# Recurrence of a hybrid trunk on whole two-head tiles, with its operands made on GpSimd

## Chip, cores and metric

The kernel runs on one core of a Trainium2 chip. The metric is the device time of one execution in microseconds; the number given for a kernel is the median of its runs.

## What is computed

Two layers of one trunk run over 256 context and 512 latent tokens of width 1024. Each layer projects the normalised tokens once and feeds three mixers (attention, a bidirectional recurrence, a short convolution); then comes a mixture of experts. The change concerns the recurrence. For each of 8 heads of width 64 and both directions, token by token:

```python
def step(s, inp):
    wt, kkt, at, kt, vt = inp[:5]
    sa = jnp.einsum('bhvk,bhk->bhv', s, kkt)
    s = s * wt[:, :, None, :] - sa[..., None] * (kkt * at)[:, :, None, :] + vt[..., None] * kt[:, :, None, :]
    y = jnp.einsum('bhvk,bhk->bhv', s, inp[5]) if emit else None
    return s, y
```

`wt` is a decay, `kkt` a normalised removal key, `at` a rate, `kt` and `vt` key and value, the last input the receptance.

## The kernel before

The 768 tokens are cut into 12 chunks of 64. Two heads (a "pair") share the 128 partitions, 64 each, and both directions `d` lie beside each other in a tile; so a layer has 4 pairs x 12 chunks = 48 steps. A step has two parts.

`window` (L639) does what needs no state, three steps ahead of its use. It makes the scaled operands `t1`, `t2` and `kr` on VectorE (L666 to L673), puts keys (`kbd`, L681) and corrections (`cbd`, L682) into two block tiles per direction, and a scaled copy of `kr` into `sv` on GpSimd (L686). Products of `kbd` and `cbd` with `kr` go to PSUM and from there, masked, into `sv` and `sc` (L700 to L709). Four transposes of the block tiles are copied to `tok` (L717 to L719). A ladder of six levels of 16-bit products (L730 to L757) then makes the inverse `xt`.

`chain` (L771) takes the state from chunk to chunk. Value and state rows of both heads lie in `V`. Each head's half is a product of its own with 64 weight columns (L794 to L797): `zz` from `V`; its copy `zr`; `aa` from `xt`; its copy `sa`; a correction of `zz`; a second `zr` and `aa`; V is overwritten (L824); `pss` gives the next state, `yy` the output, again in halves (L829 to L842). The next state is `pss` plus the decayed old one, `sf` from GpSimd (L787, L846).

`rwkv_phase` (L891) calls `ahead`, which moves three windows on by three stages each, then `chain`, then `fill`, which hands out dense projection work (`pw` products, with operands split by ScalarE, L132, and GpSimd, L134) behind marked products of the chain. The order on each engine is fixed when the program is built, by priorities (chain 9000, windows and fill 4000, dense products 0) and a modelled timeline. TensorE, VectorE, ScalarE and GpSimd each run their list in that order. An f32 product appears in the trace as two instructions, so one `mm` of two directions is a group of four.

`value_rows` (L762) copies the value rows of the next chunk into one of three `V` buffers on GpSimd; `readout` (L857) normalises the outputs of a segment on VectorE.

Of the kernel before, what the change touches and what calls it, by code (L numbers as in the profile page):

```python
# [67 lines left out]
class Trunk:  # L68
# [186 lines left out]
    def masks(self, mk):  # L255
# [3 lines left out]
        self.scm = cp.tile([P, 2, 2, P], BF16, name="scm")  # L259
# [5 lines left out]
        same, a, b = (mk.tile([P, P], F32, name=n) for n in ("mk_s", "mk_a", "mk_b"))  # L265
# [9 lines left out]
        blk(same, 6)  # L275

        for d in range(2):
            for m, op in enumerate(((ALU.is_lt, ALU.is_le), (ALU.is_gt, ALU.is_ge))[d]):
                v.tensor_tensor(a, rr, rc, op)
                v.tensor_tensor(self.scm[:, d, m], a, same, ALU.mult)  # L280
        self.scc = cp.tile([P, 2, 2, 64], BF16, name="scc")
        for h in range(2):
            hs = slice(64 * h, 64 * h + 64)
            v.tensor_copy(self.scc[hs], self.scm[hs, :, :, hs])
# [10 lines left out]
    def layer_params(self, l, pp, ps, tag):  # L295
# [24 lines left out]
        v.tensor_copy(a["c1"], cols[:, R_KA:R_KA + 4])  # L320
# [180 lines left out]
    def pair(self, p, full):  # L501
# [55 lines left out]
        def rates(s):  # L557
# [10 lines left out]
            for d in range(2):  # L568
# [16 lines left out]
                v.tensor_scalar(ta[:, d], ta[:, d], 0.5, 0.5, ALU.mult, ALU.add)  # L585
# [53 lines left out]
    def window(self, q, n, emit, kb):  # L639
# [50 lines left out]

        g.sc = rp.tile([P, 2, 2, P], F32, name="sc", tag="sc", bufs=4)
        bank = self.slots[n % 3]
        ps = bank.rearrange("p (t d m i) -> p t d m i", t=2, d=2, m=2)
# [7 lines left out]
        hi = lambda t: t.rearrange("p d m (h i) -> p d m h i", h=2)[:, :, :nm]  # L701
        if emit:
            hi = lambda t: t.rearrange("p d m (h i) -> p (d m) h i", h=2)
            in0 = ps[:, 1].rearrange("p d m i -> p (d m) i")[:, :, None].to_broadcast([P, 4, 2, 64])
            v.tensor_tensor(hi(g.sc), in0, hi(self.scm), ALU.mult)
        else:
            hi = lambda t: t[:, :, 0].rearrange("p d (h i) -> p d h i", h=2)
            in0 = ps[:, 1, :, 0, None].to_broadcast([P, 2, 2, 64])
            v.tensor_tensor(hi(g.sc), in0, hi(self.scm), ALU.mult)  # L709
        if n < NCH - 1:  # L710

            g.tok = rp.tile([P, 2, 2, 64], F32, name="tok", tag="tok", bufs=4)
            pt = bank.rearrange("p (d q x) -> p d q x", d=2, q=4)
            self.mark()
            for d in range(2):
                for t, rows in enumerate((cbd, kbd)):
                    self.tr(bank[:, (2 * d + t) * P:(2 * d + t + 1) * P], rows[:, d])  # L717
            nc.scalar.activation(g.tok[0:64], pt[0:64, :, 0::3], AF.Copy)
            nc.scalar.activation(g.tok[64:128], pt[64:128, :, 2:0:-1], AF.Copy)  # L719
# [51 lines left out]
    def chain(self, q, n, V, emit):  # L771
# [19 lines left out]
        pz = self.psz.tile([P, 2, 2, HD], F32, name="pz", tag="z")  # L791
        zz, aa = pz[:, 0], pz[:, 1]
        self.mark()
        for h, hs in enumerate(halves):  # L794
            first = self.mma(zz[hs, 0], g.sv[:, 0, h, 0], V[:, 0, h], True)
            with tc.issue_after(first.ins):
                self.mma(zz[hs, 1], g.sv[:, 1, h, 0], V[:, 1, h])  # L797
        py = self.psz.tile([P, 2, 2, HD], F32, name="py", tag="y")
        pss, yy = py[:, 0], py[:, 1]
        sa = None  # L800
        for it in range(2):
            r = rp.tile([P, 2, HD], F32R, name="zr", tag="zr", bufs=2)
            if it:
                v.tensor_tensor(r, zz, sa, ALU.subtract)
            else:
                nc.scalar.activation(r, zz, AF.Copy)
# [3 lines left out]
            if not it:  # L810
# [3 lines left out]
                for d in range(2):  # L814
                    self.mma(zz[:, d], g.sc[:, d, 0], sa[:, d])
                if emit:

                    firsts = []
                    for h, hs in enumerate(halves):
                        firsts.append(self.mma(yy[hs, 0], g.sv[:, 0, h, 1], V[:, 0, h], True))  # L820
                        with tc.issue_after(firsts[-1].ins):
                            self.mma(yy[hs, 1], g.sv[:, 1, h, 1], V[:, 1, h])
        for h, hs in enumerate(halves):
            v.tensor_copy(V[hs, :, h], aa[hs])  # L824
# [4 lines left out]
        for h, hs in enumerate(halves):  # L829
            if last:  # L830
                break
            if emit:
                with tc.issue_after(firsts[h].ins):
                    for d in range(2):
                        self.mma(pss[hs, d], g.tok[:, d, h], V[:, d, h])
            else:
                first = self.mma(pss[hs, 0], g.tok[:, 0, h], V[:, 0, h], True)
                with tc.issue_after(first.ins):
                    self.mma(pss[hs, 1], g.tok[:, 1, h], V[:, 1, h])
        if emit:  # L840
            for d in range(2):
                self.mma(yy[:, d], g.sc[:, d, 1], sa[:, d])  # L842
        if not last:
            for h, hs in enumerate(halves):
                if n:
                    v.tensor_tensor(out[hs, :, h], pss[hs], sf[hs], ALU.add)  # L846
                else:
                    v.tensor_copy(out[hs, :, h], pss[hs])
        if emit:
# [4 lines left out]
            nc.scalar.activation(ysl, yy, AF.Copy)  # L854
# [36 lines left out]
    def rwkv_phase(self, full):  # L891
        nc, tc = self.nc, self.tc
        with ExitStack() as st:
# [5 lines left out]
            kb = [[self.rp.tile([P, 2, P], F32, name=f"{n}{a}") for n in ("kbd", "cbd")] for a in range(2)]  # L899
            for t in sum(kb, []):  # L900
# [39 lines left out]
            def ahead(n, steps):  # L940

                for j in range(max(steps)):
                    for a, m in enumerate(steps):
# [3 lines left out]
                        if n + a not in gens:  # L947
                            gens[n + a] = self.window(q, c, full or c >= 4, kb[c % 2])
# [987 lines left out]
```

## Time and profile before

| | before |
|---|---|
| median of 3 runs | 3748.26 us (3740.76 to 3754.14) |
| profiled execution | 3755.7 us, of it span 3753.9 us |
| TensorE busy, weight loads busy | 3485.4 us (93%), 2313.5 us (62%) |
| VectorE, ScalarE, GpSimd busy | 2025.0 (54%), 1284.2 (34%), 893.0 us (24%) |
| mean granted TensorE clock | 0.952 of full speed |

The span runs from the first to the last instruction. PE is TensorE's products, PEld its weight loads, DVE VectorE, ACT ScalarE, POOL GpSimd. Busy is the time in which an engine had at least one instruction in work; a product counts from its start to its last result, so products overlap.

### The profile page before, as it was taken

What the parts mean: (1) busy time and instruction counts of PE and PEld (TensorE: products, weight loads), DVE (VectorE), ACT (ScalarE), POOL (GpSimd) and SP (SyncE); (2) the same over time, 40 slices, a digit from 0 to 9 for tenths busy, and PEclk for the clock granted to TensorE, in tenths of its full rate; (3) what the DMA queues carried; (4) which work ended last, traced back from release to release, by engine and by line L of the source; (5) the groups of instructions that cost most, each with busy time, mean ns of one, the idle gap of its engine ahead of it and who ended that gap; (6) DMA issues with size and microseconds to landing.
All of it is one profiled execution on the core that took longest, in us unless ns stands there. A gap on an engine that the chain in (4) does not pass through costs nothing. (4 is left out here: it accounts for less than half of the span.)

```text
span 3753.9 us, 58688 instructions
## 1 busy us (share of the span) xinstructions
PE 3485.4 (93%) x22479; PEld 2313.5 (62%) x22479; DVE 2025.0 (54%) x4902; ACT 1284.2 (34%) x3145; POOL 893.0 (24%) x1181
## 2 busy tenths in 40 slices
PE   6999999999998998999999899899999989799998
PEld 4777777777987892233333467677777978633442
DVE  6787878773665461121222677878773766412122
ACT  3454444443444211111110344555553452211111
POOL 3333343332320420000000243334343312100000
PEclk9999999999999998999999899898999999899999
DMA  5312031334115435778888411111112135399998
GB/s 177 102 61 95 29 111 49 110 114 150 52 39 183 136 133 211 294 293 310 331 331 328 138 57 29 31 36 38 35 38 92 46 132 186 132 409 409 409 409 351
DMA packets 297053, 621.11 MB, mean 165 GB/s; under 512 B 19258, under 2 KB 160532, under 8 KB 296772
## 3 DMA queue, kind: packets, MB, share of 16 engines
q1 hardware_dynamic: 293028, 605.30, 44.5%
q0 software_dynamic: 1728, 6.29, 0.5%
q10 hardware_dynamic: 2016, 5.77, 0.4%
q8 instruction: 177, 2.90, 0.3%
q14 instruction: 104, 0.85, 0.1%
HBM read 584.00 MB, written 33.29 MB: 164 GB/s over the span
## 5 line engine op out<-in xcount | busy, mean ns | idle before, releaser
L81 PE MATMUL ph<-we,xin 128*64 128x512 f32 x2048 | 514.8, 607 | 7.7 <-DMA we<-in_exp_w 4.7
L81 PE MATMUL pw<-hhi,w_hi 128*128 128x512 f32 (+1 forms) x1272 | 500.0, 397 | 14.5 <-ACT w_hi L132 6.3
L81 PE MATMUL pw<-hlo,w_hi 128*128 128x512 f32 (+1 forms) x1272 | 457.3, 364 | 0.0
L81 PE MATMUL pw<-hhi,w_lo 128*128 128x512 f32 (+1 forms) x1272 | 455.9, 364 | 1.0 <-POOL w_lo L134 1.0
L134 POOL TENSOR_TENSOR w_lo<-w_raw,w_hi 128x1024 fp32r<-128x1024 f32 x124 | 302.3, 2444 | 413.4 <-ACT w_hi L132 340.9
L81 PEld LDWEIGHTS ph<-we,xin 128*64 128x64 f32 x2048 | 151.5, 139 | 330.5 <-issue 315.7
L736 DVE TENSOR_TENSOR wt<-slot,lvm 128x256 f16<-128x256 f32 x576 | 232.8, 418 | 114.3 <-PE slot L81 78.8
L81 PEld LDWEIGHTS pw<-hhi,w_hi 128*128 128x128 f32 x1272 | 245.5, 195 | 55.2 <-ACT w_hi L132 7.6
L81 PEld LDWEIGHTS pw<-hhi,w_lo 128*128 128x128 f32 x1272 | 244.9, 194 | 38.9 <-issue 3.8
L81 PEld LDWEIGHTS pw<-hlo,w_hi 128*128 128x128 f32 x1272 | 246.2, 195 | 32.8 <-issue 13.8
L132 ACT ACTIVATE w_hi<-w_raw 128x1024 fp32r<-128x1024 f32 x168 | 177.1, 1057 | 239.4 <-DMA w_raw<-in_w_in 63.3
L81 PE MATMUL py<-we,hT 128*64 128x512 f32 x1024 | 248.5, 607 | 8.0 <-DMA we<-in_exp_w 2.8
L1791 POOL TENSOR_TENSOR ylo<-y,yhi 128x512 fp32r<-128x512 f32 x28 | 35.3, 1280 | 891.6 <-ACT yhi L1790 891.6
L753 ACT ACTIVATE xx<-slot 128x256 f16<-128x256 f32 x384 | 145.7, 382 | 166.0 <-PE slot L81 154.2
L1801 DVE TENSOR_TENSOR xr<-xr,psc 128x512 f32<-128x512 f32 x144 | 90.3, 682 | 196.6 <-PE psc L81 196.4
L1718 ACT ACTIVATE sl<-ph 64x512 f32<-64x512 f32 x64 | 37.8, 590 | 451.5 <-PE ph L81 431.8
L1719 DVE TENSOR_TENSOR hid<-sl,ph 64x512 f32<-64x512 f32 x64 | 44.2, 690 | 267.2 <-ACT sl L1718 266.7
L81 PE MATMUL slot<-xt,wt 128*128 128x128 f16 x960 | 135.9, 229 | 34.8 <-DVE wt L736 34.3
L81 PEld LDWEIGHTS py<-we,hT 128*64 128x64 f32 x1024 | 70.2, 137 | 151.6 <-issue 132.7
L81 PE MATMUL pt<-w_hi,hhi 128*128 128x256 f32 x544 | 156.2, 289 | 4.8 <-ACT xk L1115 2.0
L768 POOL COPY V<-vt 64x128 f32<-64x128 f32 x192 | 58.1, 305 | 425.3 <-PE py L85 323.0
L81 PE MATMUL pt<-w_lo,hhi 128*128 128x256 f32 x544 | 155.7, 287 | 3.2 <-POOL w_lo L134 3.2
(418 smaller groups left out, 7779.9 us busy)
## 6 DMA issues: line engine op xcount, KB each, us to landing
we<-in_exp_w SPq DMA_DIRECT2D x384, 1024.0 KB
w_raw<-in_w_in SPq DMA_DIRECT2D x124, 512.0 KB
ada_w<-in_ada_w SPq DMA_DIRECT2D x96, 512.0 KB
w_raw<-in_w_branch SPq DMA_DIRECT2D x24, 512.0 KB
w_raw<-in_w_out SPq DMA_DIRECT2D x20, 512.0 KB
gd<-gt SPq DMA_DIRECT2D x24, 384.0 KB
g<-gd SPq DMA_DIRECT2D x24, 384.0 KB
gd<-gt SPq DMA_DIRECT2D x24, 256.0 KB
```

What stands on the lines that cost most here:

```text
L81: return self.leg(self.nc.tensor.matmul(out, lhsT, rhs, start=start, stop=stop))
L132: nc.scalar.activation(hi, raw, AF.Copy)
L134: self.lo_eng.tensor_tensor(lo, raw, hi.bitcast(F32), ALU.subtract)
L736: v.tensor_tensor(wt, ps, self.lvm[:, :, l], ALU.mult)
L753: nc.scalar.activation(x, ps2, AF.Copy)
L768: self.nc.gpsimd.tensor_copy(t[ho, :, h], self.two(q.vt[s][ho], z0, z1))
L1718: nc.scalar.activation(sl, ph[0:64, ns], AF.Silu)
L1719: v.tensor_tensor(hid[0:64, ns], sl, ph[64:128, ns], ALU.mult)
L1791: (v if by_block else self.ylo_eng[nh]).tensor_tensor(lo, yn, hi.bitcast(F32), ALU.subtract)
L1801: v.tensor_tensor(x, x, pt, ALU.add)
```

## The change

The keys and corrections of a direction share one block tile `kc`; `kr` becomes a tile with one block per head, so one product per direction gives both `sv` and `sc`. `kc`, `kr` and `sc` are allocated once and cleared once, where the pool made `kr` and `sc` anew. `t1`, `t2` and `kr` are made on GpSimd. The minus sign of the corrections moves into the rates. In the chain, one product per direction takes `V` of both heads, and the block of interest is copied: `zr` per head (ScalarE and VectorE, the second time both on VectorE), `V` on VectorE and ScalarE, `y` by two ScalarE copies. The diff, cut to its core:

```diff
...
+                for h in range(2):
+                    hs = slice(64 * h, 64 * h + 64)
+                    v.tensor_copy(self.scc[hs, d, m], a[hs, hs])
...
-        v.tensor_copy(a["c1"], cols[:, R_KA:R_KA + 4])
+        v.tensor_scalar(a["c1"], cols[:, R_KA:R_KA + 4], -1.0, None, ALU.mult)
...
-                v.tensor_scalar(ta[:, d], ta[:, d], 0.5, 0.5, ALU.mult, ALU.add)
+                v.tensor_scalar(ta[:, d], ta[:, d], -0.5, -0.5, ALU.mult, ALU.add)
...
-        v.tensor_tensor(t1, t1, at(e3, True), ALU.mult)
+        pl = nc.gpsimd
+        pl.tensor_tensor(t1, t1, at(e3, True), ALU.mult)
         t2 = rp.tile(shp, F32, name="t2", tag="t2")
-        v.tensor_tensor(t2, th, at(e3, True), ALU.mult)
-        kr = rp.tile([P, 2, 2, 64], F32, name="kr", tag="kr", bufs=2)
-        v.tensor_tensor(kr[:, :, 0], kk, at(e, False), ALU.mult)
+        pl.tensor_tensor(t2, th, at(e3, True), ALU.mult)
+
+
+        kc, kr, g.sc = kb
         if emit:
             self.need(q.u["receptance"])
-            v.tensor_tensor(kr[:, :, 1], two(q.r), at(e, True), ALU.mult)
+        for h in range(2):
+            hs = slice(64 * h, 64 * h + 64)
+            pl.tensor_tensor(kr[hs, :, h, 0], kk[hs], at(e, False)[hs], ALU.mult)
+            if emit:
+                pl.tensor_tensor(kr[hs, :, h, 1], two(q.r)[hs], at(e, True)[hs], ALU.mult)
...
-        kbd, cbd = kb
         for h in range(2):
             hs, ho = slice(64 * h, 64 * h + 64), slice(64 - 64 * h, 128 - 64 * h)
-            v.tensor_tensor(kbd[hs, :, ho], two(q.k)[hs], t1[hs], ALU.mult)
-            v.scalar_tensor_tensor(cbd[hs, :, hs], kk[hs], -1.0, t2[hs], ALU.mult, ALU.mult)
-            dst = g.sv[hs, :, h, :nm]
+            v.tensor_tensor(kc[hs, :, ho], two(q.k)[hs], t1[hs], ALU.mult)
+            v.tensor_tensor(kc[hs, :, hs], kk[hs], t2[hs], ALU.mult)
+            dst = g.sv[hs, :, :nm, h]
             if n:
                 f = q.f[hs, :, n - 1, None, None].to_broadcast([64, 2, nm, 64])
-                nc.gpsimd.tensor_tensor(dst, kr[hs, :, :nm], f, ALU.mult)
+                pl.tensor_tensor(dst, kr[hs, :, h, :nm], f, ALU.mult)
             else:
-                nc.gpsimd.tensor_copy(dst, kr[hs, :, :nm])
+                pl.tensor_copy(dst, kr[hs, :, h, :nm])
...
+        ps = bank.rearrange("p (d h m i) -> p d h m i", d=2, h=2, m=2)
         self.mark()
-        for t, lhs in enumerate((kbd, cbd)):
-            for d in range(2):
-                self.mm(ps[:, t, d, :nm], lhs[:, d], kr[:, d, :nm], True, True)
+        for d in range(2):
+            self.mm(ps[:, d, :, :nm], kc[:, d], kr[:, d, :, :nm], True, True)
         for h in range(2):
-            ho = slice(64 - 64 * h, 128 - 64 * h)
-            v.tensor_tensor(g.sv[ho, :, h, :nm], ps[ho, 0, :, :nm], self.scc[ho, :, :nm], ALU.mult)
...
+            hs, ho = slice(64 * h, 64 * h + 64), slice(64 - 64 * h, 128 - 64 * h)
+            v.tensor_tensor(g.sc[hs, :, :nm, hs], ps[hs, :, h, :nm], self.scc[hs, :, :nm], ALU.mult)
+            v.tensor_tensor(g.sv[ho, :, :nm, h], ps[ho, :, h, :nm], self.scc[ho, :, :nm], ALU.mult)
...
+            g.tok = rp.tile([P, 2, P], F32, name="tok", tag="tok", bufs=4)
+                self.tr(bank[:, d * P:(d + 1) * P], kc[:, d])
+            nc.scalar.activation(g.tok, bank[:, 0:256].rearrange("p (d x) -> p d x", d=2), AF.Copy)
...
+        own = list(enumerate(halves))
+        both = lambda t, d: t[:, d, None].to_broadcast([P, 2, HD])
+        pz = self.psz.tile([P, 512], F32, name="pz", tag="z")
+        zz = pz[:, 0:256].rearrange("p (d h x) -> p d h x", d=2, h=2)
+        aa = pz[:, 256:384].rearrange("p (d x) -> p d x", d=2)
+        py = self.psz.tile([P, 2, 2, 2, HD], F32, name="py", tag="y")
+        pss, yy = py[:, 0], py[:, 1]
+
+        def begin(out, lhs):
+
+            first = self.mma(out[:, 0], lhs(0), V[:, 0], True)
+            with tc.issue_after(first.ins):
+                self.mma(out[:, 1], lhs(1), V[:, 1])
+            return first
+
...
+        begin(zz, lambda d: g.sv[:, d, 0])
+        sa = first = None
...
+            for h, hs in own:
+                if it:
+                    v.tensor_tensor(r[hs], zz[hs, :, h], sa[hs], ALU.subtract)
+                elif h:
+                    v.tensor_copy(r[hs], zz[hs, :, h])
+                else:
+                    nc.scalar.activation(r[hs], zz[hs, :, h], AF.Copy)
...
+                    self.mma(zz[:, d], g.sc[:, d, 0], both(sa, d))
...
+                    first = begin(yy, lambda d: g.sv[:, d, 1])
+        for h, hs in own:
+            if h:
+                nc.scalar.activation(V[hs, :, h], aa[hs], AF.Copy)
+            else:
+                v.tensor_copy(V[hs, :, h], aa[hs])
...
+        tok = lambda d: g.tok[:, d]
+        if last:
+            pass
+        elif emit:
+            with tc.issue_after(first.ins):
+                for d in range(2):
+                    self.mma(pss[:, d], tok(d), V[:, d])
+        else:
+            begin(pss, tok)
...
+                self.mma(yy[:, d], g.sc[:, d, 1], both(sa, d))
...
+            for h, hs in own:
...
+                    v.tensor_tensor(out[hs, :, h], pss[hs, :, h], sf[hs], ALU.add)
...
+                    v.tensor_copy(out[hs, :, h], pss[hs, :, h])
...
+            for h, hs in own:
+                nc.scalar.activation(ysl[hs], yy[hs, :, h], AF.Copy)
...
-            kb = [[self.rp.tile([P, 2, P], F32, name=f"{n}{a}") for n in ("kbd", "cbd")] for a in range(2)]
-            for t in sum(kb, []):
+            kc, kr, sc = (
+                [self.rp.tile(shape, F32, name=f"{n}{a}") for a in range(m)]
+                for n, m, shape in (("kc", 2, [P, 2, P]), ("kr", 2, [P, 2, 2, 2, 64]), ("sc", 4, [P, 2, 2, P]))
+            )
+            for t in kr + sc:
...
-                            gens[n + a] = self.window(q, c, full or c >= 4, kb[c % 2])
+                            gens[n + a] = self.window(q, c, full or c >= 4, (kc[c % 2], kr[c % 2], sc[(n + a) % 4]))
```

## Rows read from the trace of the kernel before

**Rows 1.** Stages: busy us (instructions) by engine, PEclk, DMA share, GB/s.
```profile
117.00:899.00 782.00, 740.86 (x5867) 576.92 (x5865) 578.55 (x1500) 361.19 (x1027) 266.05 (x409) 0.97 0.27 87
...
2188.00:2851.00 663.00, 610.67 (x4577) 461.47 (x4574) 506.12 (x1345) 333.68 (x949) 243.60 (x399) 0.93 0.12 37
```
**Rows 2.** First copy of each step, line 806, first layer: ns min/median/max, first and last.
```profile
L806 ACT ACTIVATE zr<-pz x48: 253/277/325, 116.9 to 898.9; 128x128 fp32r<-128x128 f32 x48
```
**Rows 3.** Timeline of one step, 2836 to 2842: start, us, instruction [idle before].
```profile
2836.79 0.60 DVE L824 COPY V<-pz 64x128 f32<-64x128 f32 x2
...
2837.49 0.45 PE L85 MATMUL py<-V,tok 128*64 128x64 f32 x4
...
2838.44 0.39 PE L81 MATMUL pw<-hhi,w_lo 128*128 128x512 f32 x1
...
2838.76 0.31 PEld L85 LDWEIGHTS py<-V,tok 128*64 128x64 f32 x4 [0.36 <-issue]
...
2839.83 0.61 DVE L846 TENSOR_TENSOR V<-py,sf 64x128 f32<-64x128 f32 x2 [2.45 <-PE py L85]
...
2840.17 0.45 PE L85 MATMUL pz<-V,sv 128*64 128x64 f32 x4 [0.26 <-DVE V L846]
...
2841.44 0.13 PEld L85 LDWEIGHTS pz<-V,sv 128*64 128x64 f32 x1 [0.37 <-issue]
```
**Rows 4.** Groups of weight loads, whole run: busy us, mean ns | idle before, releasers.
```profile
L85 PEld LDWEIGHTS pz<-V,sv 128*64 128x64 f32 x768 | 54.5, 142 | 52.6 <-issue 9.6 <-DVE V L848 9.6 <-DVE V L846 8.3
...
L85 PEld LDWEIGHTS pz<-sa,sc 128*128 128x128 f32 x384 | 53.8, 200 | 4.8 <-ACT xt L757 1.5 <-issue 0.8 <-ACT sa L812 0.7
...
L85 PEld LDWEIGHTS py<-V,tok 128*64 128x64 f32 x704 | 51.6, 141 | 35.3 <-issue 11.7 <-DVE V L824 5.2 <-DVE wt L736 4.6
```
**Rows 5.** Timeline of TensorE's products, 400 to 415 us.
```profile
402.81 0.70 PE L81 MATMUL bk<-wal,ups 64*128 64x256 f32 x2
...
406.16 0.46 PE L85 MATMUL py<-V,sv 128*64 128x64 f32 x8
...
407.72 0.27 PE L108 MATMUL slot<-ident,kbd 128*128 128x128 f32 x1
...
409.84 0.61 PE L85 MATMUL pz<-sa,sc 128*128 128x64 f32 x4
...
411.86 0.61 PE L81 MATMUL slot<-kr,cbd 128*128 128x128 f32 x4
```
**Rows 6.** VectorE in the window: groups of the whole run, and one line's ns min/median/max.
```profile
L682 DVE SCALAR_TENSOR_TENSOR cbd<-kk,t 64x128 f32<-64x128 f32 x192 | 92.2, 480 | 19.9 <-PE slot L108 17.9
...
L700 DVE TENSOR_TENSOR sv<-slot,scc 64x256 f32<-64x256 f32 (+1 forms) x192 | 76.6, 399 | 42.9 <-PE slot L81 38.5 <-PE pz L85 0.8 <-ACT sa L827 0.4
...
L705 DVE TENSOR_TENSOR sc<-slot,scm 128x512 f32<-128x512 f32 x80 | 54.5, 682 | 1.4 <-PE py L85 0.5
...
L670 DVE TENSOR_TENSOR kr<-kk,e 128x128 f32<-128x128 f32 x96 | 37.2, 387 | 1.7 <-POOL sv L686 0.2
...
L682 DVE SCALAR_TENSOR_TENSOR cbd<-kk,t x192: 270/290/2532, 99.1 to 2802.4; 64x128 f32<-64x128 f32 x192
```
**Rows 7.** GpSimd products of 128x128 and 64x128: ns min/median/max, first and last start.
```profile
L1132 POOL TENSOR_TENSOR rot<-xq,r_q x32: 445/459/903, 976.3 to 3042.9; 128x128 f32<-128x128 f32 x32
...
L787 POOL TENSOR_TENSOR sf<-V,f x160: 392/399/960, 176.4 to 2841.0; 64x128 f32<-64x128 f32 x160
```
**Rows 8.** Timeline of all engines, 2571 to 2576 us.
```profile
2571.89 2.34 POOL L134 TENSOR_TENSOR w_lo<-w_raw,w_hi 128x1024 fp32r<-128x1024 f32 x1
...
2572.24 2.70 DVE L874 TENSOR_SCALAR var<-var 128x16 f32<-128x16 f32 x1
...
2575.18 0.69 PE L85 MATMUL pz<-V,sv 128*64 128x64 f32 x4 [2.15 <-DVE V L848]
```
**Rows 9.** GpSimd's copy of value rows, second recurrence phase: busy us, mean ns | idle before.
```profile
L768 POOL COPY V<-vt 64x128 f32<-64x128 f32 x90 | 27.7, 307 | 206.5 <-PE py L85 144.6 <-DVE wt L736 22.8 <-DVE V L824 19.7
```

More of the change, by code (lines that the diff above doesn't have):

```diff
@@ L258, in masks @@
         v = nc.vector
-        self.scm = cp.tile([P, 2, 2, P], BF16, name="scm")
         self.lvm = cp.tile([P, 2, 6, P], F16, name="lvm")
@@ L264, in masks @@
         rc, rr, ci, ri = (mk.tile([P, P], I32, name=n) for n in ("mk_c", "mk_r", "mk_ci", "mk_ri"))
-        same, a, b = (mk.tile([P, P], F32, name=n) for n in ("mk_s", "mk_a", "mk_b"))
+        a, b = (mk.tile([P, P], F32, name=n) for n in ("mk_a", "mk_b"))
         nc.gpsimd.iota(rc, pattern=[[1, P]], base=0, channel_multiplier=0)
@@ L273, in blk @@
             v.tensor_tensor(dst, ci, ri, ALU.is_equal)
-        blk(same, 6)
+        self.scc = cp.tile([P, 2, 2, 64], BF16, name="scc")
         for d in range(2):
@@ L279, in masks @@
                 v.tensor_tensor(a, rr, rc, op)
[L280 to L284, printed above, removed]
+                for h in range(2):
+                    hs = slice(64 * h, 64 * h + 64)
+                    v.tensor_copy(self.scc[hs, d, m], a[hs, hs])
         for l in range(6):
@@ L684, in window @@
+            dst = g.sv[hs, :, :nm, h]
             if n:
                 f = q.f[hs, :, n - 1, None, None].to_broadcast([64, 2, nm, 64])
-                nc.gpsimd.tensor_tensor(dst, kr[hs, :, :nm], f, ALU.mult)
+                pl.tensor_tensor(dst, kr[hs, :, h, :nm], f, ALU.mult)
             else:
-                nc.gpsimd.tensor_copy(dst, kr[hs, :, :nm])
+                pl.tensor_copy(dst, kr[hs, :, h, :nm])
         yield
-        g.sc = rp.tile([P, 2, 2, P], F32, name="sc", tag="sc", bufs=4)
@@ L701, in window @@
[L701 to L709, printed above, removed]
+            hs, ho = slice(64 * h, 64 * h + 64), slice(64 - 64 * h, 128 - 64 * h)
@@ L710, in window @@
+            v.tensor_tensor(g.sc[hs, :, :nm, hs], ps[hs, :, h, :nm], self.scc[hs, :, :nm], ALU.mult)
+            v.tensor_tensor(g.sv[ho, :, :nm, h], ps[ho, :, h, :nm], self.scc[ho, :, :nm], ALU.mult)
         if n < NCH - 1:
-            g.tok = rp.tile([P, 2, 2, 64], F32, name="tok", tag="tok", bufs=4)
-            pt = bank.rearrange("p (d q x) -> p d q x", d=2, q=4)
+            g.tok = rp.tile([P, 2, P], F32, name="tok", tag="tok", bufs=4)
             self.mark()
             for d in range(2):
-                for t, rows in enumerate((cbd, kbd)):
-                    self.tr(bank[:, (2 * d + t) * P:(2 * d + t + 1) * P], rows[:, d])
@@ L789, in chain @@
                 )
-        pz = self.psz.tile([P, 2, 2, HD], F32, name="pz", tag="z")
-        zz, aa = pz[:, 0], pz[:, 1]
-        self.mark()
[L794 to L800, printed above, removed]
+        own = list(enumerate(halves))
[10 more added lines that the diff above has]
+            return first
+        self.mark()
+        begin(zz, lambda d: g.sv[:, d, 0])
+        sa = first = None
         for it in range(2):
             r = rp.tile([P, 2, HD], F32R, name="zr", tag="zr", bufs=2)
[L803 to L806, printed above, removed]
+            for h, hs in own:
[5 more added lines that the diff above has]
+                    nc.scalar.activation(r[hs], zz[hs, :, h], AF.Copy)
             self.mark()
@@ L814, in chain @@
                 for d in range(2):
-                    self.mma(zz[:, d], g.sc[:, d, 0], sa[:, d])
+                    self.mma(zz[:, d], g.sc[:, d, 0], both(sa, d))
                 if emit:
[L818 to L824, printed above, removed]
+                    first = begin(yy, lambda d: g.sv[:, d, 1])
[4 more added lines that the diff above has]
+                v.tensor_copy(V[hs, :, h], aa[hs])
         if emit:
@@ L828, in chain @@
         self.mark()
[L829 to L839, printed above, removed]
+        tok = lambda d: g.tok[:, d]
[7 more added lines that the diff above has]
+            begin(pss, tok)
         if emit:
             for d in range(2):
-                self.mma(yy[:, d], g.sc[:, d, 1], sa[:, d])
+                self.mma(yy[:, d], g.sc[:, d, 1], both(sa, d))
         if not last:
-            for h, hs in enumerate(halves):
+            for h, hs in own:
                 if n:
-                    v.tensor_tensor(out[hs, :, h], pss[hs], sf[hs], ALU.add)
+                    v.tensor_tensor(out[hs, :, h], pss[hs, :, h], sf[hs], ALU.add)
                 else:
-                    v.tensor_copy(out[hs, :, h], pss[hs])
+                    v.tensor_copy(out[hs, :, h], pss[hs, :, h])
         if emit:
```

4 lines of the change are left out of this document (removed).

## The prediction

> **What bounds the kernel now.** I read the stages first, then the recurrence inside them, then what its links wait for.
>
> The stage table [rows 1] has one line for each recurrence phase, 117 to 899 us in the first layer and 2188 to 2851 in the second. TensorE is busy for 741 of 782 us and 611 of 663, VectorE for 579 and 506, ScalarE for 361 and 334, GpSimd for only 266 and 244. So TensorE and VectorE are the full engines, and GpSimd has the room. All of the change lies in these two phases, 1445 us together.
>
> A phase is 48 steps (four head pairs, twelve chunks) [rows 2]: 782 us over 47 intervals are 16.6 us a step, 663 are 14.1. TensorE is not 93% full of work, though: a lone small product counts as busy until it has drained, and in these phases dense projection products are put between the links of the chain. The handoffs show what that does [rows 3]. The second V copy ends at 2837.39 (2836.79 + 0.60), but the second half of the state product starts at 2838.76, 1.37 us later, because dense products stand between the halves. The next link has the same shape: the second half of the new state is there at 2840.44, its product starts at 2841.44, 1.00 us later. And each of these second halves has 0.36 or 0.37 us of idle weight load in front of it, put down to "issue". Over the run, the weight loads of `pz<-V,sv` and `py<-V,tok` have 52.6 and 35.3 us of idle in front of them, against 4.8 for the full-width `pz<-sa,sc` [rows 4]. So the step is a chain of short links, each queued in an engine's fixed order; it is not one engine's throughput.
>
> **The change part by part**, per step.
>
> *TensorE, the products with V.* `zz` and `pss` are today two pieces of four instructions, 0.45 us each [rows 3]; each becomes one piece of four with 128 weight columns and 128 moving columns, for which the nearest row is `slot<-kr,cbd`, 0.61 us [rows 5]. That saves 0.29 us twice. `yy` stands in one piece of eight at 0.46 [rows 5] and becomes 0.61: +0.15. Of the idle before the half-width loads, 87.9 us / 96 = 0.92 a step, part is a true wait for V (the rows name it); I take 0.4 off, between 0 and 0.88.
>
> *TensorE, the rest.* The corrections `sc` times `sa` go from 64 to 128 moving columns. At 64 columns four take 0.61 us, and at 128 columns four of `kr,cbd` take 0.61 as well [rows 5]: nothing. The window's eight products of 128 columns become four of 256. Streaming the same columns gives 0 as one end; the other is `bk<-wal,ups`, two of 256 columns in 0.70 [rows 5], so four in 1.40 against 2 x 0.61: +0.2. I take +0.1. Two of four transposes go: (0.61 - 0.27) / 3 = 0.11 between starts [rows 5], so -0.22. The sum for TensorE is -0.58 + 0.15 - 0.4 + 0.1 - 0.22 = -0.95 us, with ends at -1.7 and +0.15.
>
> *The chain.* Each of `zz` and `pss` now waits for both halves and then goes at once. The 1.00 and 1.37 us between the halves can go wholly (-2.4), or not at all if the dense products land in front of the merged product instead. I take -0.9. Against it, the second `zr` is two VectorE copies in a row instead of one (+0.30, half of a pair's 0.60 in rows 3), the V copies run side by side on two engines (-0.30), and three handoffs now need VectorE and ScalarE both free. I take +0.3 for the three, between 0 and +1. Net -0.6.
>
> *VectorE.* Four operand products leave. The nearest rows give 0.39 with its port waits and 0.29 without [rows 6]; 4 x 0.35 = -1.4. The block products are taken from PSUM by four instructions of 0.40 instead of two of 0.40 and one of 0.68 [rows 6]: +0.12. `zr` costs two copies more and V one less: +0.30. That is -1.0. What can eat it is the port: the `cbd` copies take 480 ns in the mean and 290 in the median [rows 6], so four such instructions lose 4 x 0.19 = 0.76 us a step while GpSimd holds SBUF. That loss may stay (0) or double (+0.76); I take +0.2, so VectorE -0.8.
>
> *GpSimd.* Two products of 128x128 at 0.46 and four of 64x128 at 0.40 [rows 7] are 2.5 us a step more. In the second layer it rises from 244 / 48 = 5.1 to 7.6 us of a 14.1 us step. I cost that at nothing: a window begins three steps before it is used. If that cover is gone, its operands come 2.5 - 1.4 = 1.1 us later.
>
> *ScalarE.* One `tok` copy less; one V copy and one `y` copy more: about +0.2 us on an engine that is half idle; nothing. The masks and the cleared tiles are made once a layer, two more `memset` tiles and larger ones: under 3 us a layer on idle GpSimd; nothing. The DMA queues get no instruction more or less.
>
> *The sum.* These do not add up, since each is partly hidden by the others. I take a third of TensorE's 0.95 (the rest becomes waiting), half of the chain's 0.6 (the fixed order can put another product in its place), and a quarter of VectorE's 0.8: 0.3 + 0.3 + 0.2 = 0.8 us a step. Over 96 steps that is 77 us. The profiled execution took 3755.7 us, so 3679; the median of the runs shown, 3748.3, is 7.4 below it, so the forecast is 3671.5 for a median. With all of TensorE's and the chain's share, 1.55 us a step, it would be 149 us, about 3600.
>
> **The rivals.**
>
> *The gain is given back at the handoffs* (chance 0.22). Three links now need a VectorE and a ScalarE copy of the same product. VectorE is three quarters busy and ScalarE half [rows 1], and both work strictly in order, so the later of two queues counts. With +0.9 instead of +0.3, and dense products in front of the merged ones, the chain gains 0 and only TensorE's and VectorE's shares are left, which waiting swallows: 0 to 0.25 us a step, 3725 to 3750. For it: the step is links, not throughput. Against it: the pieces of 0.45 and the idle of 0.36 vanish whatever the copies do. I expect 3740.
>
> *Slower: GpSimd and its port become the bound* (chance 0.22). A VectorE instruction with two SBUF inputs, or one that only scales a small SBUF tile, stands still while GpSimd works: the 128x16 scaling took 2.70 us beside a `w_lo` of 2.34, and the chain's next product waited 2.15 us for the copy behind it [rows 8]. That shows the mechanism already on the chain. The Trainium skill, "SBUF — State Buffer", section "SBUF: two separate sides", has it as a rule that speaks against this change: the port pair is an exclusive lock, held for a whole instruction, and the loser blocks fully. By that rule, the trace agrees (2.70 us for an instruction that is that long only behind the lock). In this kernel it would work so: the four `kc` products come just as GpSimd makes the same window's `kr` and `sv`, each waits for one GpSimd instruction of 0.40 [rows 7], 1.6 us, and holds GpSimd up for 4 x 0.29 = 1.2 us [rows 6]. GpSimd then has 7.6 + 1.2 = 8.8 us a step, and its fixed order parks it: 206.5 us of the second layer, 4.3 us a step, it stands before the V copy of a later step [rows 9]. 8.8 + 4.3 = 13.1 us, just what the shorter step would be (14.1 - 0.8 = 13.3). From there the windows come late and TensorE stands before their products: the window's path is 1.1 + 1.6 = 2.7 us longer, and half of that, less the 0.8 gained, is +0.55 us a step: 3748 + 53 = 3801, about 3795. Against it: the parked time shrinks by itself when GpSimd has something else in front, and VectorE keeps only five such instructions of nine a step.
>
> *The change doesn't do what it says* in one point: the chain's matrix products lose instructions, not columns. That is in the sum already.
>
> **How the numbers follow.** Forecast 3672 (0.56), its own band 3600 to 3725; the handoff rival 3740 (0.22), which covers 3725 to 3760; the port rival 3795 (0.22), from 3760 up. About 0.3%, 11 us, is what a measurement of this kernel can tell from no change, so faster begins below 3737: all of the forecast and nearly half of the handoff rival, 0.66. Same takes the rest of it, 0.12; slower is the port rival, 0.22. The range that holds 8 in 10 leaves out the forecast's lowest end (below 3600, 0.08) and half of the port rival (above 3790, 0.11).
>
> **What would show each step right or wrong.** Right: `pz` and `py` products with V in one piece of four per link, with no "issue" idle before them; the two phases shorter by 35 to 45 us each; VectorE some 40 us less busy in each, GpSimd some 120 us more; `kc` at 480 ns or less in the mean. The port rival would show in `kc` above 700 ns, in long scalings beside GpSimd, and in TensorE waiting for `nb` or `kc`. The handoff rival would show in phases of the old length, with `zr` and V waiting for whichever copy comes second. The forecast is wrong if the phases are not shorter although the pieces merged, or if the gain lies outside 117 to 899 and 2188 to 2851.

## The result and the profile after

The changed kernel takes 3643.94 us (median of 4 runs, 3639.78 to 3644.71) against 3744.70 us for the kernel before on the same chip: a ratio of 0.9722, 95% interval 0.9709 to 0.9734; that is 101 us less by the medians and 104 by the ratio. The profiled execution has a span of 3641.9 us where it was 3753.9.

Busy time over the whole run, from the page of the changed kernel; the clock beside it is 0.963:

```profile
PE 3367.1 (92%) x20863; PEld 2243.8 (62%) x20863; DVE 1950.3 (54%) x4725; ACT 1289.5 (35%) x3233; POOL 1133.7 (31%) x1729
```

The stage table of the changed kernel, for the two recurrence phases (from the first to the last `zr` copy), answers to [rows 1]. Columns: length, then busy time of TensorE, weight loads, VectorE, ScalarE and GpSimd, then granted clock and DMA:

```profile
118.00:845.00 727.00, 689.90 (x5032) 550.63 (x5032) 542.24 (x1419) 366.47 (x1078) 378.71 (x674) 0.99 0.29 94
2138.00:2741.00 603.00, 538.48 (x3775) 414.05 (x3774) 470.82 (x1261) 326.85 (x977) 348.15 (x636) 0.97 0.13 40
sum 1330.00, PE 1228.38 PEld 964.69 DVE 1013.05 ACT 693.32 POOL 726.85; mean PE 614.19 PEld 482.34 DVE 506.53 ACT 346.66 POOL 363.43
```

The phases went from 782 to 727 and from 663 to 603 us. That is 115 us of 1445, or 1.2 us a step, and it is the whole gain: the stretch between them lasts 1293 us, before 1289. VectorE is 36 and 35 us less busy, GpSimd 113 and 105 us more, TensorE 51 and 72 us less. TensorE's idle time did not shrink: 1445 - 1351.5 = 93 us before, 1330 - 1228.4 = 102 now.

TensorE's busy time is not work alone. Its mean granted clock, 0.97 and 0.93 in [rows 1], is now 0.99 and 0.97 in the two phases. In the traces' records of the clock, 140 us of the two phases stood at the lower of its two levels (1.2 of 2.4 GHz) before, in 25 stretches, and 61 us now, in 12; each stretch came behind a time in which TensorE had stood idle in part. At half clock at most half of the time is lost, so by this estimate 70 us were lost before and 31 now: up to 39 of the 115 us can have come by the clock.

The groups of the changed kernel that answer to [rows 4, 6, 7], whole run: busy us, mean ns, idle before and what ended it:

```profile
L81 PE MATMUL slot<-kr,kc 128*128 128x256 f32 (+1 forms) x384 | 97.5, 376 | 1.5 <-ACT xtr L746 1.0
L674 POOL TENSOR_TENSOR kr<-kk,e 64x128 f32<-64x128 f32 x192 | 91.7, 477 | 109.0 <-PE slot L81 78.8 <-DVE kk L545 19.8 <-DVE vt L634 1.9
L684 DVE TENSOR_TENSOR kc<-kk,t 64x128 f32<-64x128 f32 x192 | 78.6, 409 | 5.9 <-POOL t L666 5.4
L683 DVE TENSOR_TENSOR kc<-pk,t 64x128 f32<-64x128 f32 x192 | 78.3, 408 | 16.1 <-PE slot L108 9.6 <-POOL t L664 3.5 <-PE slot L81 0.7
L85 PEld LDWEIGHTS pz<-V,sv 128*128 128x128 f32 x384 | 50.4, 190 | 35.2 <-PE slot L81 24.5 <-DVE V L844 3.4 <-PE py L85 1.9
L85 PEld LDWEIGHTS py<-V,tok 128*128 128x128 f32 x352 | 47.4, 194 | 12.2 <-ACT V L822 10.6 <-issue 0.3
...
L666 POOL TENSOR_TENSOR t<-a,e 128x128 f32<-128x128 f32 x96 | 43.6, 455 | 55.1 <-DVE kc L684 49.8 <-ACT xx L742 2.0 <-ACT sa L827 0.9
L805 DVE CAST zr<-pz 64x128 fp32r<-64x128 f32 x96 | 28.3, 295 | 18.1 <-ACT zr L807 15.5
L822 ACT ACTIVATE V<-pz 64x128 f32<-64x128 f32 x96 | 26.2, 273 | 47.2 <-DVE V L824 45.0
```

The block products are hardly slower beside a busier GpSimd: 0.41 us, against 0.37 and 0.39 in e1 below, where GpSimd does as little as before (0.48 and 0.43 in the kernel before, where one of the two kinds was another instruction). The idle before the weight loads of the products with V fell from 87.9 to 47.4 us, and "issue" no longer leads it: what stands first is a product in front or the copy of V. The last two lines show something new: of each pair of split copies, the second waits for the first.

One step of the changed kernel in its timeline, where [rows 3] has the step of before (start, us, instruction, idle before):

```profile
2727.76 0.28 DVE L824 COPY V<-pz 64x128 f32<-64x128 f32 x1
...
2728.56 0.27 ACT L822 ACTIVATE V<-pz 64x128 f32<-64x128 f32 x1
...
2728.89 0.71 PE L85 MATMUL py<-V,tok 128*128 128x128 f32 x4 [0.22 <-ACT V L822]
...
2730.78 0.61 DVE L844 TENSOR_TENSOR V<-py,sf 64x128 f32<-64x128 f32 x2 [2.74 <-PE py L85]
...
2731.54 0.68 PE L85 MATMUL pz<-V,sv 128*128 128x128 f32 x4 [0.68 <-DVE V L844]
...
2732.26 0.27 ACT L807 ACTIVATE zr<-pz 64x128 fp32r<-64x128 f32 x1 [0.22 <-PE pz L85]
2732.56 0.29 DVE L805 CAST zr<-pz 64x128 fp32r<-64x128 f32 x1 [0.71 <-ACT zr L807]
```

Each product with V is now one piece that starts 0.06 and 0.15 us after the last V value is there, where the second halves started 1.37 and 1.00 us late. But the copies stand one behind the other: `zr` 2732.26 and then 2732.56, V 2727.76 and then 2728.56 (ScalarE had another copy in front).

### The profile page after: what moved, and what is told of

It reads as the page before. It is cut to its first block, busy times and chain, and to the rows that moved or that the text cites. A ratio compares the mean times of both kernels' runs of the same rounds, so it can differ in the third digit from the quotient of the medians.

```text
span 3641.9 us, 56218 instructions
## 1 busy us (share of the span) xinstructions
PE 3367.1 (92%) x20863; PEld 2243.8 (62%) x20863; DVE 1950.3 (54%) x4725; ACT 1289.5 (35%) x3233; POOL 1133.7 (31%) x1729
## 4 chain that ended last, share of the span: by engine, by line
PE 50%; DVE 9%; DMA 2%; ACT 2%; issue 2%; POOL 1%; DVEq 0%; ACTq 0%; POOLq 0%
PE ph L81 13%; PE pw L81 6%; PE py L81 6%; PE pc L81 4%; PE po L81 3%; PE slot L81 2%; PE pt L81 2%; PE psc L81 2%; PE pyc L81 2%; PE ba L81 2%; PE pz L85 2%; DMA we<-in_exp_w 2%; PE py L85 1%; PE pxi L81 1%; DVE wt L725 1%
## 5 line engine op out<-in xcount | busy, mean ns | idle before, releaser
L81 PE MATMUL pw<-hhi,w_hi 128*128 128x512 f32 (+1 forms) x1272 | 490.7, 390 | 15.0 <-ACT w_hi L132 6.7
L81 PE MATMUL pw<-hlo,w_hi 128*128 128x512 f32 (+1 forms) x1272 | 451.2, 359 | 0.0
L81 PE MATMUL pw<-hhi,w_lo 128*128 128x512 f32 (+1 forms) x1272 | 450.9, 360 | 0.3 <-POOL w_lo L134 0.3
L81 PE MATMUL pt<-w_hi,hlo 128*128 128x256 f32 x544 | 154.7, 285 | 0.0
```

Source lines behind the costliest of these rows:

```text
L81: return self.leg(self.nc.tensor.matmul(out, lhsT, rhs, start=start, stop=stop))
```

## The experiments

The change has three parts: operands on GpSimd, the chain on whole tiles, and the merged tile `kc`. The first six kernels take them apart.

**e1**: the changed kernel, operands back on VectorE.

```diff
-        pl.tensor_tensor(t1, t1, at(e3, True), ALU.mult)
+        v.tensor_tensor(t1, t1, at(e3, True), ALU.mult)
...
-            pl.tensor_tensor(kr[hs, :, h, 0], kk[hs], at(e, False)[hs], ALU.mult)
+            v.tensor_tensor(kr[hs, :, h, 0], kk[hs], at(e, False)[hs], ALU.mult)
```

> The changed kernel with the six operand products of the window (t1, t2, four for kr) back on VectorE; all else as changed. Before 3744.7, changed 3643.9 us. Theory (the merged products of the chain carry the gain, VectorE's relief a third of it): 3675, so 30 us given back. Rival (VectorE's relief is nearly the whole gain): 3725 or more. Rival (GpSimd's port takes back what VectorE saves): 3645 or less. VectorE's busy time in the two phases rises by 6 x 0.29 us x 96 = 165 us less what its other copies stop waiting for GpSimd.

**e2**: the changed kernel with the chain per head of before (`sv` and `tok` indexed in the new order).

```diff
+        for h, hs in enumerate(halves):
+            first = self.mma(zz[hs, 0], g.sv[:, 0, 0, h], V[:, 0, h], True)
...
-        begin(zz, lambda d: g.sv[:, d, 0])
...
```

> The changed kernel with the chain as before it: products with V per head with 64 weight columns, one copy for zr, V and y each as before. Window and GpSimd operands as changed. Theory (the chain carries two thirds): 3710 us, with about 90 us of idle again before the half-width weight loads. Rival (VectorE's relief carries it): 3660 or less. Rival (fewer window products carry it): 3660 or less, with the idle before the half-width loads back all the same.

**e3**: the kernel before, with only `t1`, `t2` and `kr` on GpSimd (as e1, the other way round).

> The kernel before with one thing alone: t1, t2 and kr made on GpSimd (four products of 128x128). Theory: 3715 us, 30 less than before. Rival (VectorE's relief is nearly all): 3665 or less. Rival (the port of GpSimd): 3745 or more, with the kbd and cbd products above 500 ns in the mean.

**e4**: the kernel before with only the new chain.

```diff
-        for h, hs in enumerate(halves):
-            first = self.mma(zz[hs, 0], g.sv[:, 0, h, 0], V[:, 0, h], True)
...
+        begin(zz, lambda d: g.sv[:, d, 0])
```

> The kernel before with one thing alone: the chain's products over whole tiles, with their copies per head. Window as before, all on VectorE. Theory: 3680 us, 65 less than before, and the idle before the loads of V's products falls from 88 us to under 30. Rival (VectorE is the bound): 3745 or more, since VectorE gets three copies more and one less a step. Rival (the gain needs both parts): 3730.

**e5**: only the merged tile: e2 with e1's edit. **e12**: the change without the merged tile: e4 with e3's edit.

> Of the change only the merged tile of corrections and keys (one weight load and one 256-column product per direction) is left; the chain is per head and the operands are made on VectorE, both as before. Theory (each part's gain hangs on how much VectorE has left to do in the two recurrence phases, and the merged tile is worth the same wherever it stands): it was worth 34 us between e3 and e2 and 38 us between e4 and e1, so 3748 - 36 = about 3712 us, with VectorE 20 to 30 us less busy in the phases. Rival (the merged tile pays through TensorE's pieces and needs VectorE relieved first, as the chain does): 3735 to 3750 us.

> The change without the merged tile of corrections and keys: operands on GpSimd and the chain of whole tiles, on the window of before; it is the last corner of the eight ways to take three parts. From the other seven (operands alone -31, chain alone +22, tile alone -3; tile with operands -31 more than the sum, tile with chain -34 more) the whole change's -101 asks for -24 between operands and chain if parts work only in pairs: 3748 - 31 + 22 - 24 = about 3715 us. Rival (all three are needed at once, the chain gains nothing without the tile): 3735 to 3745 us. Rival (the operands alone free the chain, the tile adds little): 3670 to 3690 us.

All eight ways to take the three parts, each with its ratio to the kernel before on its own chip; the last four columns are us in the two phases together (TensorE idle is length less busy):

| operands on | chain | tile | ratio to before [95%] | length | TensorE busy | VectorE busy | TensorE idle |
|---|---|---|---|---|---|---|---|
| VectorE | halves | two (before) | 1 | 1445 | 1352 | 1085 | 93 |
| VectorE | halves | one (e5) | 0.9992 [0.9982, 1.0001] | 1427 | 1321 | 1115 | 106 |
| VectorE | whole | two (e4) | 1.0053 [1.0027, 1.0079] | 1459 | 1309 | 1112 | 150 |
| VectorE | whole | one (e1) | 0.9955 [0.9938, 0.9971] | 1414 | 1256 | 1127 | 158 |
| GpSimd | halves | two (e3) | 0.9915 [0.9892, 0.9939] | 1411 | 1334 | 999 | 77 |
| GpSimd | halves | one (e2) | 0.9822 [0.9797, 0.9847] | 1367 | 1298 | 978 | 69 |
| GpSimd | whole | two (e12) | 0.9832 [0.9816, 0.9848] | 1375 | 1263 | 1008 | 112 |
| GpSimd | whole | one (after) | 0.9722 [0.9709, 0.9734] | 1330 | 1228 | 1013 | 102 |

In us of some 3745: with the operands on VectorE, the new chain costs 20, the merged tile gives 3, and both give 17. With them on GpSimd (32 gained by that alone), the chain gives 31 more, the tile 35 more, and both 72 more. So with the operands on GpSimd chain and tile about add up. With them on VectorE they do not: alone they come to -17 us, together to +17. The chain needs one of the other two parts: it costs 20 us alone and gives 14 on top of the tile (e5 to e1). The tile too: it gives 3 us alone, but 37 on top of the chain with the operands still on VectorE (e4 to e1). The table's last columns show part of how. On VectorE's side of the table, chain and tile take 95 us of busy time from TensorE (1352 to 1256), and 64 us of it come back as idle time. On GpSimd's side they take 106 (1334 to 1228) and 25 come back. The clock goes along: at the lower level stood 154 us of the two phases in e4, 99 in e1, 79 in e12 and 61 in the changed kernel. No run holds the clock fixed, so how much of a step in the table is work and how much is clock stays open; and why the tile pays on top of the chain where VectorE is no less busy (1112 to 1127 us) is not shown. Against what was on record, by the medians: e1 (3732 us) and e4 (3770) went the way of the rivals that name VectorE; e3 (3717) went as the theory said; e2 (3683) lies between its theory and its rivals; e5 (3743) went with its rival; e12 (3683) has the number of its last rival but not its reason, since the tile still adds 41 us to it.

e4 loses in the second phase (697 us against 663 before; its first is 20 us shorter). What TensorE's products wait for there, in e4 and then in the kernel before (us in total, times, longest):

```profile
PE slot L81 <- DVE wt L736: 41.2, 33, 3.7
PE pz L85 <- DVE V L855: 12.0, 26, 0.8
PE pz L85 <- DVE zr L814: 9.3, 11, 2.0
...
PE pz L85 <- DVE zr L816: 6.2, 8, 1.8
PE py L85 <- ACT V L833: 6.1, 9, 1.8
```

```profile
PE slot L81 <- DVE wt L736: 22.9, 20, 2.8
PE pz L85 <- DVE V L848: 7.7, 4, 3.0
...
PE pz L85 <- DVE V L846: 3.1, 8, 0.8
```

`wt` is the masked product of the inverse's ladder. It does not belong to the chain, but it stands in the same fixed order of VectorE as the chain's copies, of which the new chain has one more a step, and the window's products. More of the idle time lies at the handoffs. Over both phases, all waits for copies of `zr` and V come to 22 us before, 62 in e4, 86 in e1, 54 in e12 and 41 in the changed kernel; those for `wt` to 37, 52, 29, 21 and 22. Most of these copies are VectorE's. So the new chain makes TensorE wait for VectorE's copies, and the move of the operands takes part of that wait away again (62 to 54 us without the tile, 86 to 41 with it).

**e6**: the changed kernel, but each product with V again one instruction per head, with 128 weight columns.

```diff
-            first = self.mma(out[:, 0], lhs(0), V[:, 0], True)
+            first = self.mma(out[:, 0, 0], lhs(0), V[:, 0, 0], True)
             with tc.issue_after(first.ins):
-                self.mma(out[:, 1], lhs(1), V[:, 1])
+                self.mma(out[:, 1, 0], lhs(1), V[:, 1, 0])
+                for d in range(2):
+                    self.mma(out[:, d, 1], lhs(d), V[:, d, 1])
...
```

> As after with full-width weights and the wait for both halves, but each product with V is again one instruction per head (64 columns), so the pieces have eight instructions and four weight loads for four and two; VectorE, ScalarE and GpSimd do what they do in after. Theory TensorE (the merged chain pays by TensorE's shorter pieces once VectorE has room): TensorE 60 to 90 us more busy in the phases, 3665 to 3700 us. Rival (it pays by the idle before half-width loads, which stays away here, or by the single start): 3640 to 3655 us.

Measured: 3716.95 us, ratio 0.9926 [0.9910, 0.9943], some 75 us more than the changed kernel. Its phases, and the groups with V (mean 191 ns for a load, 272 for a product of 64 columns, against 142 and 240 with half-width weights in e2):

```profile
sum 1401.00, PE 1326.29 PEld 1076.27 DVE 1010.80 ACT 700.61 POOL 725.88; mean PE 663.14 PEld 538.13 DVE 505.40 ACT 350.31 POOL 362.94
```

```profile
L85 PE MATMUL pz<-V,sv 128*128 128x64 f32 x768 | 112.3, 272 | 7.7 <-DVE V L847 3.0 <-DVE V L849 2.6 <-ACT sa L829 1.1
...
L85 PEld LDWEIGHTS pz<-V,sv 128*128 128x128 f32 x768 | 103.5, 191 | 23.4 <-DVE V L847 10.6 <-DVE V L849 3.9 <-ACT sa L829 1.9
```

VectorE is as busy as in the changed kernel (1011 against 1013 us), TensorE 98 us more, and the phases are 71 us longer. So with VectorE relieved, TensorE's work is time; the clock is not the cause here, since e6 has less time at the lower level (44 us) than the changed kernel (61). The single wait for both halves and the missing idle before half-width loads are both kept in e6, and it still loses: what pays is that one instruction, with one weight load, does both heads.

**e7**: the changed kernel, both copies of the first `zr` on ScalarE, both of V on VectorE. **e9**: all four on ScalarE. The edit shown is e7's.

```diff
-                elif h:
-                    v.tensor_copy(r[hs], zz[hs, :, h])
...
-            if h:
-                nc.scalar.activation(V[hs, :, h], aa[hs], AF.Copy)
-            else:
-                v.tensor_copy(V[hs, :, h], aa[hs])
+            v.tensor_copy(V[hs, :, h], aa[hs])
```

> As after, but both copies of the first zr on ScalarE and both copies of V on VectorE, so no handoff between the two engines within a pair; VectorE's busy time stays the same within 3 us. Theory (the split copies are one behind the other, since both read one PSUM bank, and each pair costs a handoff of some 0.2 us on the chain): 0.4 us a step less on the chain, of which about half shows: 3615 to 3630 us against 3644. Rival (chain latency is covered by other work in most steps, only VectorE's load counts): 3640 to 3650 us.

> As after, but the copies of the first zr and of V are all on ScalarE: VectorE loses 2 instructions a step (0.30 and 0.28 us, 55 us in all over 96 steps), ScalarE gains as many, and no pair changes engines. Theory VectorE (0.4 to 0.75 us of time for each us of its load): 3600 to 3622 us. Theory handoff (as e7, whatever VectorE does): within 5 us of e7. Rival (ScalarE, 52 per cent busy in the phases, becomes late, three copies stand in a row ahead of yy): 3640 to 3665 us.

Measured: e7 3653.14 us (0.9753 [0.9737, 0.9769]), e9 3641.98 us (0.9712 [0.9691, 0.9734]), beside 0.9722 for the changed kernel. The line below is e9's two phases. Taking the handoff out of the pairs does not pay: e7 is about 10 us slower, e9 the same. e7 lies outside both of its ranges, and only 2 us of its loss are in the phases (1332 us; VectorE is 10 us busier there, not within 3). So the change of engine within a pair is no loss that counts. The two copies still stand one behind the other in both kernels, so what a side-by-side copy would be worth is not tested. e9 misses the handoff theory (it is 11 us from e7) and the theory that each us of VectorE's load is time: VectorE is 43 us less busy in the phases and ScalarE 50 more. But e9's four runs have a lower clock (0.959 to 0.963, the changed kernel's 0.963 to 0.965), and 85 us of its phases stand at the lower level, not 61; by the estimate above that can hide up to 12 us.

```profile
sum 1327.00, PE 1223.90 PEld 973.02 DVE 969.94 ACT 742.87 POOL 732.99; mean PE 611.95 PEld 486.51 DVE 484.97 ACT 371.44 POOL 366.49
```

**e11**: the changed kernel and, beside it, products of a constant on VectorE that nobody reads.

```diff
+        load = rp.tile([P, P], F32, name="load", tag="load")
+        for hs in [slice(0, P)] * 2 + [slice(0, 64), slice(64, P)] * (2 if emit else 1):
+            v.tensor_tensor(load[hs], self.ident[hs], self.ident[hs], ALU.mult)
```

> As after, operands on GpSimd, but VectorE also makes the six products of e1 once more from a constant tile into a scratch tile that nobody reads: its load is e1's (about 114 us more in the phases), the path of the operands is after's. Theory VectorE load (what the move to GpSimd buys is room in VectorE's queue): near e1, 3715 to 3750 us. Rival path (it pays because the window's operands are made beside the chain and are ready earlier): 3640 to 3665 us.

Measured: 3757.20 us (1.0038 [1.0024, 1.0053]): all of the gain is gone and more, a little beyond the theory's range. But it is not the test that was meant. Having no inputs to wait for, the products were put at the front of each phase when the order was fixed: 288 of 544 run from 63 to 267 us and take 108 us, the others from 2139 to 2333 us and take 104. First e11's stages there, then the changed kernel's:

```profile
100.00:200.00 100.00, 83.27 (x456) 62.27 (x456) 95.32 (x252) 30.95 (x75) 41.91 (x69) 0.88 0.23 72
...
2140.00:2340.00 200.00, 159.45 (x794) 117.29 (x793) 188.08 (x494) 69.52 (x177) 88.22 (x157) 0.83 0.12 36
```

```profile
100.00:200.00 100.00, 96.84 (x635) 74.62 (x634) 69.29 (x161) 42.15 (x114) 56.13 (x97) 1.00 0.30 95
...
2140.00:2340.00 200.00, 175.39 (x1189) 134.11 (x1187) 161.08 (x422) 105.04 (x313) 116.18 (x214) 0.93 0.13 38
```

With VectorE 95% busy, TensorE gets 456 products through where it had 635. The fifth step of the first phase starts 57 us later than in the changed kernel, the last one 59 (904.0 against 844.7): once the load is past, nothing more is lost. In the second phase 104 us of load cost 50 more. So this VectorE time that nobody waits for costs about half of itself. TensorE's clock falls with it, to 0.88 and 0.83 in these stages. Whether load spread over all steps costs the same, e11 cannot say.

**e8**: the changed kernel, the four `kc` products on GpSimd too. **e10**: e8 and e9 together.

```diff
-            v.tensor_tensor(kc[hs, :, ho], two(q.k)[hs], t1[hs], ALU.mult)
-            v.tensor_tensor(kc[hs, :, hs], kk[hs], t2[hs], ALU.mult)
+            pl.tensor_tensor(kc[hs, :, ho], two(q.k)[hs], t1[hs], ALU.mult)
+            pl.tensor_tensor(kc[hs, :, hs], kk[hs], t2[hs], ALU.mult)
```

> As after, but the four products that fill the merged tile of corrections and keys are on GpSimd too (4 of 0.41 us a step off VectorE, about 157 us of busy time). Theory (VectorE's load in the phases is the bound, about 0.75 us of time for each us of it, as e1 gave back 88 us for 114 us): 3540 to 3590 us. Rival 1 (GpSimd and VectorE share a port and the operands get longer by their being made one after another on GpSimd): 3640 to 3680 us, with GpSimd's products above 0.5 us mean or its share of the phases above 0.75. Rival 2 (VectorE's load no longer binds after the change): 3625 to 3645 us.

> e8 and e9 together: the products of the merged tile on GpSimd, the copies of zr and V on ScalarE. Theory VectorE load (43 us less of it, as in e9): 3580 to 3600 us. Rival, as e9 showed against after: ScalarE's 50 us more give it back, within 8 us of e8's 3613.

Measured: e8 3612.59 us, 0.9638 [0.9622, 0.9654]; e10 3597.96 us, 0.9608 [0.9592, 0.9624]. Both beat the changed kernel, e8 by 31 us and e10 by some 45. Phases of e8 and, in the second fence, of e10; then GpSimd's groups of e8:

```profile
sum 1303.00, PE 1219.39 PEld 962.20 DVE 904.21 ACT 695.63 POOL 907.53; mean PE 609.70 PEld 481.10 DVE 452.11 ACT 347.81 POOL 453.76
```

```profile
sum 1275.00, PE 1200.24 PEld 952.85 DVE 861.78 ACT 740.64 POOL 902.65; mean PE 600.12 PEld 476.42 DVE 430.89 ACT 370.32 POOL 451.33
```

```profile
L684 POOL TENSOR_TENSOR kc<-kk,t 64x128 f32<-64x128 f32 x192 | 94.4, 492 | 17.8 <-DVE kk L545 15.4
L683 POOL TENSOR_TENSOR kc<-pk,t 64x128 f32<-64x128 f32 x192 | 94.0, 489 | 18.7 <-PE slot L81 6.0 <-PE slot L108 2.8
...
L729 DVE TENSOR_TENSOR xt<-nb,lvm 128x256 f16<-128x256 f16 x96 | 52.1, 543 | 9.9 <-POOL nb L715 8.9
```

The rival of e11, that the operands are ready earlier beside the chain, is settled by the products that use them first. Their groups in the kernel before and in e1, both with the operands on VectorE:

```profile
L81 PE MATMUL slot<-kr,kbd 128*128 128x128 f32 (+1 forms) x384 | 67.6, 296 | 0.9 <-DVE kbd L681 0.8
L81 PE MATMUL slot<-kr,cbd 128*128 128x128 f32 (+1 forms) x384 | 63.2, 287 | 0.0
```

```profile
L81 PE MATMUL slot<-kr,kc 128*128 128x256 f32 (+1 forms) x384 | 99.5, 382 | 0.5 <-ACT xtr L746 0.5
```

TensorE stood 0.9 and 0.5 us before them in a whole run, and 1.5 in the changed kernel. The operands were never late, so there was nothing to gain by having them earlier. What e8 adds is room on VectorE, which is 109 us less busy for 31 us of time. That is less than the 0.75 us for each us that was expected, and TensorE is 94% busy again. GpSimd is 70% busy (908 of 1303 us), and TensorE's products wait directly for it for 0.3 us in the two phases. e10 takes another 42 us from VectorE and gains 11 to 15 us, with intervals that touch; the same edit alone (e9) gained nothing that can be measured. e10 has 31 us of its phases at the lower clock level, e8 48, so part of the difference between the two results can be clock; whether the edit pays only on top of e8 is open.

## Why the prediction was right, and where not

The forecast was 3672 us in a range from 3600 to 3790; it came to 3644. By its steps:

- **Where the gain lies.** Right: all of it in the two phases. They are 55 and 60 us shorter, not 35 to 45. The result lies in a range that was 190 us wide; the gain in the phases was half as large again as forecast, 115 us against 77.
- **The work moved.** VectorE's -0.8 us a step measured (1013 - 1085) / 96 = -0.75. GpSimd's rise of 120 a phase measured 113 and 105, and no run shows a cost of it, as argued; its parked time before the V copy, 206.5 us in [rows 9], shrank to 66.7, which the rival's counter-argument had said. The 0.4 us of idle taken off the loads with V measured 40.5 / 96 = 0.42; what that is worth by itself is not shown (e6 keeps it and still loses).
- **TensorE's -0.95** was too small. Without the 0.4 of idle before loads, which is not busy time of products, -0.55 was forecast; the busy time measured (1228 - 1352) / 96 = -1.28. Of the small terms, `kc` at 256 columns was expected at +0.1 us a step; the group takes 97.5 us where the two of before took 67.6 + 63.2, a third of a us less. Part of the rest is no work taken away: the three groups of `pw`, which the change does not touch, are busy for 20 us less in all (500.0, 457.3 and 455.9 us before, 490.7, 451.2 and 450.9 now). The prediction has no term for the clock.
- **Slips in its working** that move nothing: TensorE's ends of -1.7 and +0.15 do not come out of its listed terms, which give -1.53 and -0.45; and the port rival's sum is 3801, not 3795.
- **The chain: V copies "side by side on two engines (-0.30)".** Wrong. Both copies read one product, and the second waits for the first (45.0 of the 47.2 us of idle before `V` on ScalarE, 15.5 of the 18.1 before `zr` on VectorE). What that cost is not measured: e7 and e9 only take the change of engine away. Of the chain's terms one has a number: three dearer handoffs were taken at +0.3 us a step, and TensorE's waits for copies of `zr` and V rose by (41 - 22) / 96 = 0.2.
- **The step that failed: the sum.** It took fixed shares, a third of TensorE, half of the chain, a quarter of VectorE, 0.8 us a step in all, and 1.2 were measured. These runs show no fixed share. With operands on VectorE, 95 us less TensorE work made the phases 31 us shorter (before to e1), just the third that was taken; with operands on GpSimd, 106 us made them 81 shorter (e3 to after), three quarters. Nor is a full VectorE all that decides: from e4 to e1, with VectorE no less busy, 53 us less TensorE time made the phases 45 us shorter. VectorE's relief of 86 us gave 34 alone (before to e3), and 114 us gave 84 with the other two parts in place (e1 to after). The parts pay in company: any two gave more than the two alone. The reading that VectorE and TensorE are the full engines was right; that relief of one can be kept back by the other was not drawn from it, and neither was the clock, which rose with the relief.
- **The handoff rival (3740)** describes e4 (3770) and e1 (3732), the chain without the move to GpSimd, and its mechanism is in their traces: TensorE waits 62 and 86 us for copies of `zr` and V where it was 22. It had not counted that the move of the operands would cut this to 41.
- **The port rival (3795)** is refuted twice: `kc` ran at 0.41 us with GpSimd at 727 us in the phases, and e8 loads GpSimd with 181 us more and gains. The lock is there, at the price of few long waits: 10 of the 384 `kc` products of the changed kernel took over 0.9 us at a median of 0.29, and each of them overlaps a `w_lo` of GpSimd; the longest took 2.47 us, begun 0.1 us after a `w_lo` of 2.43. The Trainium skill, "SBUF — State Buffer", section "SBUF: two separate sides", says that the loser waits for the other's whole instruction; the 2.47 us agree with that. The rule was not wrong, its price was: a wait at each of the four `kc` products a step was assumed, and the mean in the changed kernel is 0.41 us. The `wt` copies, which read PSUM and are nearly a quarter of VectorE's time in the phases (230 of 1013 us), stay at 0.42 us in all kernels. `xt`, with both inputs in SBUF, lies between 0.34 us (e6) and 0.54 (e8) in the mean, with no order by GpSimd's load.

## What to carry to other kernels

When two engines share a stage at 75% and 94%, cost a relief of one with the other as it is and as it will be after the change: here the same two parts were worth 17 us with VectorE full and 72 with VectorE relieved. Parts that lose or do nothing alone (+20, -3) can be most of the gain once another part is in, so take a change of several parts apart in all combinations before any is dropped. Read the granted clock of each stage beside the busy times: here it rose with the change, and up to a third of the gain can be its. An idle engine can take elementwise work of a full one even if each instruction is slower there (0.49 against 0.41 us).

## What the runs showed that was not expected

GpSimd's products did not go by partitions: 64x128 took 0.477 us (`kr`, L674) and 128x128 0.455 us (`t`, L666), and e3's `kr`, one instruction of 128x128, took 0.482 us. So making `kr` in halves nearly doubled its cost there. And work that waits for nothing was put first when the order was fixed (e11), where it kept TensorE's products back.
